# A hybrid decoder block on one core: another division of the first loads and of the memory's scaling, the last left half in two pieces, and another written order

## The chip, the cores and the metric

The kernel runs on one core of a Trainium2 chip. The time is device time in microseconds, the median of several executions; the profile is one further execution, recorded by the hardware profiler.

A core has five engines with a queue each. PE multiplies matrices and writes into PSUM banks. DVE (VectorE) and ACT (ScalarE) work on the elements, POOL (GpSimd) does little of that here, and SP only issues DMAs. POOL and ACT can issue DMAs too, and all of these transfers run on the same 16 DMA engines. Each engine works through its queue in the order in which the program was written, and waits at an instruction until what it reads is there.

## The reference

One layer on 512 tokens of width 1024, all in float32. Three branches read one projection of the normalised input; their gated sum goes through an output projection, then a feed-forward part with a short convolution, then a last norm.

```python
h = rmsnorm(x, norm_mix_g);  proj = h @ w_in            # 1024 x 9216
y_a = (gb * causal_conv3(gc * v)) @ w_a_out             # short gated convolution
u   = causal_conv31(u * sigmoid(ug)) + conv_b_bias      # convolution module
y_b = silu(layernorm(u)) @ w_b_out
k, vm = split(rmsnorm(mem, norm_mem_g) @ w_kv)          # 256 memory rows, 4 heads
y_c = attention(q, k, vm) @ w_att_out
x = x + (sum of sigmoid(gate_i) * y_i) @ w_o
h = rmsnorm(x, norm_ffn_g)
gt, up = split(causal_conv3(h @ w_up))                  # 1024 x 5632
x = x + (silu(gt) * up) @ w_down                        # 2816 x 1024
out = rmsnorm(x, norm_final_g)
```

## The kernel before, in words

**Precision.** A float32 operand is split into a high and a low part that PE takes at its full rate, and each product is three matmuls: high by high, high by low, low by high (`product`, L634 to L636, and `multiply`, L866). A weight therefore passes through four steps before PE can use it: the load, by SP's queue (L713) or by POOL's, which can also add to what is there (L808); the high part on ACT (`whi`, L683); the low part on DVE (`wlo`, L687); the matmuls. There are four buffers for split weights, so the high part of a unit waits until PE is through with the unit four places before it.

**Blocks.** The large projections are cut into "quads", four output blocks that are computed by seven products of sums of blocks in place of eight products. A unit, written (q, f) with f from 1 to 7, is 24 matmuls of 128 by 256. The seven units of a quad share three PSUM banks, and what lies in them is read in seven steps, r1 to r7, by ACT (L893 to L916) and DVE (`add`, L900, and `minus`, L640). Some units add onto a bank that an earlier read has to have seen: unit 6 waits for r1, unit 7 for r6, unit 4 for r7, unit 3 for r5. The usual order of units has another quad's unit between such a pair.

**Stages on PE, in order.** Eleven matmuls of no use to the result that keep PE running while the first loads come (L2105); keys and values of the memory (L1146 and on); the quads of the input projection with the attention between them; the merge of the branches; the output projection (`wo`), the transposes of the normalised rows (`tr`, L1993); eleven quads of the up projection, (up, 0) to (up, 10); the down projection; the end. In the up stage, each pair of quads gives columns of gate (gt) and value (uu). DVE and ACT apply the three taps of the convolution to them (L1654, L1660: into gtc and upc), ACT applies the silu to gtc (L2090), DVE multiplies (z, L2073), and z is split into zh and zl (L2274) for the down projection.

**What sets the order.** The program is a list of jobs (class `Jobs`), each with an engine, a cost, the jobs that it comes after and the buffers that it takes. PE's jobs have a fixed order, that of the list `seq`, in which the table `MOVES` puts single units elsewhere. For all other engines a list scheduler picks the next job by the time at which it could start and then by its due time, which is counted back from PE's order. Two tables shift this per kind of job: `LATER` adds to a due time, `AHEAD` says how long before its due time a job may start at all. `FRESH` names units whose first matmuls write their bank in another pattern. The scheduler's times only set the order; on the chip, semaphores hold each engine.

**The start.** SP loads the memory (two halves, mem), then the keys' first weights (L1081), the values' (L1081) and the next ones. ACT loads its function table (L627), issues the load of 16 columns of norm weights (pk, L628), copies the averaging matrix (mean_w, L629) and scales the four chunks of the first memory half by their norm weights (mg, L954). PE multiplies unsplit float32 there (`keys_product`, L1146), each half of it from two of the chunks.

**The end.** The last of four token blocks is added up in two halves (L2429), squared and summed (L2432), its root taken on ACT (L2453) and inverted on DVE (L2501). Then DVE scales its left 512 columns (L2463) and SP stores them, while ACT scales the right ones (L2459) and stores them on its own queue (L2468).

Of the kernel before, what the change touches and what calls it, by code (L numbers as in the profile page):

```python
# [8 lines left out]
F32 = mybir.dt.float32  # L9
F32R = mybir.dt.float32r  # L10
AF = mybir.ActivationFunctionType
# [3 lines left out]
P = 128  # L15
# [62 lines left out]
    "ACT c3": -190.4, "ACT cf": 13.1, "ACT csq": 651, "ACT exp": -246.7, "ACT fh h b00": -1,  # L78
# [4 lines left out]
    "ACT mg0": 6, "ACT mgh a": 11.9, "ACT mgh b": -6, "ACT mgh c": -22.7, "ACT mgh d": -539,  # L83
    "ACT mgh e": -123, "ACT mgh g": 4, "ACT mh": 472, "ACT mu high": 22, "ACT oh": -68.6,
    "ACT pth": -80, "ACT qh": -60.7, "ACT r1 bb": 75, "ACT r1 cv": 61.8, "ACT r1 gate": 335.4,
# [5 lines left out]
    "ACT sc": -95, "ACT sg": -4.8, "ACT sigmoid": 49, "ACT silu": 91, "ACT sq": -65, "ACT sr": -14,  # L91
    "ACT st": -0.2, "ACT swish": -944, "ACT tap 0": 323, "ACT tap 1": 95, "ACT tap 2": 5,
# [8 lines left out]
    "ACT xg": 33.2, "ACT xroot": -347, "ACT xsquare": 120, "ACT zh a": -186, "ACT zh b": -50,  # L101
    "ACT zh c": -3.4, "ACT zh e": -11, "ACT zh f": -93, "ACT zh g": -0.8, "DVE CV": 16.7,
    "DVE c3": -233, "DVE centre": 100, "DVE cf": 121.1, "DVE csum": -12, "DVE ends": -93.7,
# [6 lines left out]
    "DVE lns": -4.6, "DVE low": -427, "DVE m scale": -18, "DVE mfold": 2, "DVE mfold2": 277,  # L110
    "DVE mgl a": -2.1, "DVE mgl b": -5, "DVE mgl c": -11, "DVE mgl d": 400.7, "DVE mgl g": -334.1,
    "DVE ml": 82, "DVE ms c": -232, "DVE ms e": -2.2, "DVE ms f": 266, "DVE msum": -7,
    "DVE mu fold": -70, "DVE mu low": -150, "DVE mu sum": -187, "DVE ol": 10.7, "DVE pn": -22.2,
# [7 lines left out]
    "DVE sum": 167.8, "DVE tap 0": 898, "DVE tap 1": 336, "DVE tap 2": 0.8, "DVE tap 3": 567,  # L121
    "DVE top": -3576.1, "DVE tot1": 143.2, "DVE tot2": -268.9, "DVE v scale": 78.8,
    "DVE var fold": 114, "DVE var sum": 8, "DVE vl": -9.8, "DVE weigh": -226, "DVE wl K 0": 89.1,
# [8 lines left out]
    "DVE xn": 12.6, "DVE xnorm": -40, "DVE xsum": 40.6, "DVE y t4": -169, "DVE y t5": -5,  # L132
# [9 lines left out]
    "POOL wadd x": -1269, "POOL wadd y": 4, "POOL wl merge 0": 3.3, "POOL wl merge 2": -163.8,  # L142
# [372 lines left out]
def hybrid_block_kernel(  # L515
# [429 lines left out]
    for g in range(2):  # L945
# [1639 lines left out]
```

## Time and profile before

| | before |
| --- | --- |
| median of 3 runs | 918.65 us (918.6 to 918.81) |
| the profiled execution | 918.8 us, of which the span of the trace is 917.0 |
| PE | 908.5 us busy, 99% of the span, 6789 matmuls |
| DVE | 848.7 us, 93% |
| ACT | 684.6 us, 75% |
| POOL | 137.1 us, 15% |
| moved by DMA | 196.91 MB, 215 GB/s |
| granted TensorE clock | 0.999 |

PE is the engine that is nearly always busy, and DVE is next. A row of the timeline gives the start, the duration, the engine, the line and the tiles, and in brackets how long the engine stood idle before it and for what. A row of the waits gives who waited for whom: the sum in us, how often, the longest. A row of the DMA view ends with the size of one transfer and the time from its issue to its landing.

### The profile page before, as it was taken

To read this page: it belongs to the slowest core of one execution; us is meant where nothing else is said; L and a number is where in the kernel's file an instruction comes from. 1 tells how busy PE (TensorE), PEld (TensorE's weight loads), DVE (VectorE), ACT (ScalarE), POOL (GpSimd) and SP (SyncE) were. 2 spreads that over 40 slices of the span, in tenths; PEclk is the share of its full clock that TensorE was granted. 3 is DMA by queue.
4 is the path that set the end of the run, shared out by engine and by line. 5 is a ranking of instruction groups with operands and counts; after the bars stand their busy time and mean duration, and the time that the engine had idled before them with its cause. 6 is when DMAs were issued, how large, how long until landed. Compare 5 with 4: busy or idle time off the path is not lost.

```text
span 917.0 us, 17020 instructions
## 1 busy us (share of the span) xinstructions
PE 908.5 (99%) x6789; PEld 858.7 (94%) x6789; DVE 848.7 (93%) x965; ACT 684.6 (75%) x940; POOL 137.1 (15%) x164
## 2 busy tenths in 40 slices
PE   9999999999999999999999999999999999999997
PEld 8999999999989999999899997899999999988886
DVE  6996999999999999999898989898979899999977
ACT  7777978889988876879748874767757676765566
POOL 0021111101011121110111211121211111002210
PEclk9999999999999999999999999999999999999999
DMA  9999778746769799786958999999999687779962
GB/s 367 371 293 196 153 177 201 157 117 150 212 144 274 167 197 239 151 185 176 227 126 242 204 260 322 260 219 293 276 259 215 143 194 161 191 258 316 270 136 93
DMA packets 55377, 196.91 MB, mean 215 GB/s; under 512 B 6273, under 2 KB 6401, under 8 KB 55297
## 3 DMA queue, kind: packets, MB, share of 16 engines
q0 software_dynamic: 22608, 81.54, 49.4%
q1 hardware_dynamic: 32400, 114.02, 34.3%
q8 instruction: 53, 0.87, 0.4%
q10 hardware_dynamic: 288, 0.27, 0.1%
q14 instruction: 28, 0.22, 0.1%
HBM read 191.60 MB, written 4.19 MB: 214 GB/s over the span
## 4 chain that ended last, share of the span: by engine, by line
PE 99%; DVE 1%; issue 0%; ACT 0%; DVEq 0%
PE bank L866 65%; PE bank L634 7%; PE bank L636 7%; PE bank L635 7%; PE bank L1705 3%; PE bank L1706 3%; PE bank L1704 3%; PE bank L1157 2%; PE bank L1938 1%; PE bank L2105 1%; PE bank L1146 0%; PE bank L1400 0%; PE bank L1993 0%; PE ss L1021 0%; DVE z L2073 0%
## 5 line engine op out<-in xcount | busy, mean ns | idle before, releaser
L683 ACT CAST whi<-wf 128x1024 fp32r<-128x1024 f32 (+1 forms) x197 | 205.2, 1044 | 96.4 <-PE bank L866 48.7
L687 DVE TENSOR_TENSOR wlo<-wf,whi 128x1024 fp32r<-128x1024 f32 (+1 forms) x191 | 230.0, 1213 | 12.3 <-ACT whi L683 12.0
L1472 ACT ACTIVATE tp<-u,pk 128x511 f32<-128x511 f32 (+22 forms) x184 | 119.0, 705 | 6.9 <-DVE acc L1479 5.8
L1479 DVE TENSOR_TENSOR acc<-acc,tp 128x1022 f32<-128x1022 f32 (+22 forms) x92 | 109.4, 1191 | 8.4 <-ACT tp L1472 6.8
L808 POOL DMA_DIRECT2D wf<-in_w_in x43 | 39.4, 938 | 217.0 <-DVE wlo L687 187.2
L866 PE MATMUL bank<-ft4h,whi 128*128 128x256 f32 x248 | 68.6, 277 | 0.9 <-DVE uu L640 0.9
L866 PE MATMUL bank<-fb10h,whi 128*128 128x256 f32 x248 | 68.7, 277 | 0.0
L866 PE MATMUL bank<-fb00h,whi 128*128 128x256 f32 x248 | 68.7, 277 | 0.0
L866 PE MATMUL bank<-ft7h,whi 128*128 128x256 f32 x248 | 68.7, 277 | 0.0
L866 PE MATMUL bank<-ft5l,whi 128*128 128x256 f32 x248 | 68.7, 277 | 0.0
L866 PE MATMUL bank<-fb11h,whi 128*128 128x256 f32 x248 | 68.7, 277 | 0.0
L866 PE MATMUL bank<-ft6l,whi 128*128 128x256 f32 x248 | 68.6, 277 | 0.0
L866 PE MATMUL bank<-ft6h,whi 128*128 128x256 f32 x248 | 68.6, 277 | 0.0
L866 PE MATMUL bank<-ft6h,wlo 128*128 128x256 f32 x248 | 68.6, 276 | 0.0
L866 PE MATMUL bank<-ft7l,whi 128*128 128x256 f32 x248 | 68.6, 276 | 0.0
L866 PE MATMUL bank<-ft5h,whi 128*128 128x256 f32 x248 | 68.6, 276 | 0.0
L866 PE MATMUL bank<-ft5h,wlo 128*128 128x256 f32 x248 | 68.5, 276 | 0.0
L866 PE MATMUL bank<-ft7h,wlo 128*128 128x256 f32 x248 | 68.5, 276 | 0.0
L866 PE MATMUL bank<-fb10l,whi 128*128 128x256 f32 x248 | 68.5, 276 | 0.0
L866 PE MATMUL bank<-fb10h,wlo 128*128 128x256 f32 x248 | 68.5, 276 | 0.0
L866 PE MATMUL bank<-ft4l,whi 128*128 128x256 f32 x248 | 68.5, 276 | 0.0
L866 PE MATMUL bank<-fb00l,whi 128*128 128x256 f32 x248 | 68.5, 276 | 0.0
(418 smaller groups left out, 3172.1 us busy)
## 6 DMA issues: line engine op xcount, KB each, us to landing
wf<-in_w_in SPq DMA_DIRECT2D x50, 512.0 KB, 5.9
wf<-in_w_in POOLq DMA_DIRECT2D x43, 512.0 KB, 6.6
wf<-in_w_up SPq DMA_DIRECT2D x31, 512.0 KB, 6.9
wf<-in_w_up POOLq DMA_DIRECT2D x30, 512.0 KB, 7.2
wf<-in_w_down SPq DMA_DIRECT2D x15, 512.0 KB, 6.1
wf<-in_w_kv SPq DMA_DIRECT2D x8, 512.0 KB, 8.7
wf<-in_w_v SPq DMA_DIRECT2D x8, 512.0 KB, 8.1
wf<-in_w_att_out SPq DMA_DIRECT2D x8, 512.0 KB, 4.1
```

The costliest lines, as they stand in the source:

```text
L634: nc.tensor.matmul(ps, s_hi, w_hi, start=start, stop=False, skip_group_check=again)
L635: nc.tensor.matmul(ps, s_hi, w_lo, start=False, stop=False, skip_group_check=again)
L636: nc.tensor.matmul(ps, s_lo, w_hi, start=False, stop=stop, skip_group_check=again)
L683: nc.scalar.copy(parts[0], src())
L687: nc.vector.tensor_tensor(lo, src(), hi.bitcast(F32), op=ALU.subtract)
L808: nc.gpsimd.dma_start(out=tiles[key], in_=block(w, col[c], k), accum_op=ALU.add)
L866: nc.tensor.matmul(to, w[:, k, at], col, start=first and n == 0, stop=k == 3 and n == 2, skip_group_check=again,)
L1472: nc.scalar.activation(two(("tp", p, s))[:, j, s:], two(("u", p))[:, j, : SEQ - s], AF.Copy, scale=weight(j),)
L1479: nc.vector.tensor_tensor(a, a, two(("tp", p, s))[:, :, s:], op=ALU.add)
L1704: nc.tensor.matmul(ps, w_hi[:, i, at], hi, start=first, stop=False)
L1705: nc.tensor.matmul(ps, w_hi[:, i, at], lo, start=False, stop=False)
L1706: nc.tensor.matmul(ps, w_lo[:, i, at], hi, start=False, stop=last)
```

## The change

Five things are edited.

1. pk's load goes from ACT's queue to POOL's, where it is the first instruction of the kernel's own; the copy of mean_w goes from ACT to DVE.
2. The first load of the keys' weights goes from SP's queue to ACT's, behind the table load in the order of the program.
3. The four chunks of mg are four jobs in place of two: chunks 0 and 2 on ACT, chunks 1 and 3 on DVE. Each half of the keys' product comes after two of them.
4. The left half of the last token block is scaled and stored in two pieces of 256 columns, both by DVE and SP.
5. The tables `LATER`, `AHEAD`, `MOVES` and `FRESH` hold other entries, so the order of nearly all jobs off PE is another, and on PE the order of some units of the up stage and of three transposes.

```diff
 LATER = {
-    "ACT c3": -190.4, "ACT cf": 13.1, "ACT csq": 651, "ACT exp": -246.7, "ACT fh h b00": -1,
+    "ACT cf": 470, "ACT exp": -1067.2, "ACT fh h b00": -451, "ACT fh h b10": -0.1,
...
 FRESH = {
-    (("glu", 2), 7), (("q", 1), 5), (("bb", 0), 7), (("bb", 1), 1), (("gate", 0, 1), 2),
-    (("up", 2), 1), (("up", 0), 5), (("up", 0), 4), (("up", 1), 4), (("up", 2), 6),
+    (("glu", 2), 7), (("q", 1), 5), (("q", 1), 7), (("bb", 0), 7), (("bb", 1), 1),
+    (("gate", 0, 1), 2), (("mq", 1), 3), (("up", 0), 5), (("up", 0), 4), (("up", 1), 7),
+    (("up", 1), 4), (("up", 2), 6),
 }
 MOVES = [
...
-    ((("up", 1), 7), (("up", 1), 4)),
-    ((("up", 1), 2), (("up", 0), 5)),
-    (("tr", 0), ("tr", 1)),
+    (("tr", 2), ("tr", 3)),
+    (("tr", 0), ("wo", "g", 0, 1)),
...
 AHEAD = {
-    "ACT c3": 80, "ACT exp": 80, "ACT fh h b10": 10, "ACT fh h b11": 5, "ACT fh h t5": 10,
+    "ACT csq": 10, "ACT fh h b10": 5, "ACT fh h t4": 150, "ACT fh h t5": 20, "ACT fh h t6": 20,
...
     ident = const.tile([P, P], F32, tag="ident", name="ident")
+    eps = const.tile([P, 1], F32, tag="eps", name="eps")
+    pk = const.tile([P, N_PACKED], F32, tag="pk", name="pk")
+    nc.gpsimd.dma_start(out=pk[:, :N_GAINS], in_=packed[:, :N_GAINS])
     make_identity(nc, ident)
...
     nc.vector.memset(mean_col, 1.0 / D)
+    nc.vector.tensor_copy(mean_w, mean_col.broadcast_to([P, P]))
     nc.scalar.preload_act_table_set("sqrt_and_others")
-    nc.scalar.dma_start(out=pk[:, :N_GAINS], in_=packed[:, :N_GAINS])
-    nc.scalar.copy(mean_w, mean_col.broadcast_to([P, P]))
...
-            def mem_scaled(e=e):
-                if e == 0:
-                    make(("mg0",))
-                for i in range(2 * e, 2 * e + 2):
-                    nc.scalar.activation(
-                        four(("mg0",))[:, i, :], four(("mem", 0))[:, i, :], AF.Copy,
-                        scale=par("norm_mem_g", i),
-                    )
+            def mem_scaled(i):
+                to, t, scale = four(("mg0",))[:, i, :], four(("mem", 0))[:, i, :], par("norm_mem_g", i)
+                if i % 2:
+                    nc.vector.tensor_scalar(to, t, scale, None, op0=ALU.mult)
+                else:
+                    nc.scalar.activation(to, t, AF.Copy, scale=scale)
...
-        job(("ld0", s), "SP", LOAD, lambda: nc.sync.dma_start(out=tiles[raw], in_=src),
-            [("raw tile", s)], LOAD_LATENCY, use=[raw])
+        job(("ld0", s), "SP", LOAD, lambda: (nc.scalar if s == "K" else nc.sync).dma_start(
+            out=tiles[raw], in_=src), [("raw tile", s)], LOAD_LATENCY, use=[raw])
...
-    def left_scaled(t):
-        x1 = late["x1"][t][0]
+    def left_scaled(t, cols=slice(0, SEQ)):
+        x1 = late["x1"][t][0][:, cols]
         nc.vector.scalar_tensor_tensor(
-            x1, x1, r_fin[t], late["g"][0], op0=ALU.mult, op1=ALU.mult
+            x1, x1, r_fin[t], late["g"][0][:, cols], op0=ALU.mult, op1=ALU.mult
         )
...
+        for e, part in enumerate(ENDS if t == last else (slice(0, SEQ),)):
+            job(("sl", t, e), "DVE", 0.37 if t == last else 0.67,
+                lambda t=t, part=part: left_scaled(t, part), [("rc", t)])
+            job(("st", t, 0, e), "SP", STORE, lambda t=t, part=part: stored(t, 0, nc.sync, part),
+                [("sl", t, e)], LOAD_LATENCY)
```

Three places in the order of the program, each as it stands before and as it stands after. A row is one instruction, or several alike (x2), with its line; a number behind a tile's name only tells buffers apart.

ACT's queue at the program's start, before:

```order
L627 ACT_TABLE_LOAD
L628 DMA pk<-in_packed 128x16
L629 CAST mean_w<-mean_col 128x128
L954 ACTIVATE mg_8_118<-mem_95,pk 128x256 x4
L966 CAST mh_129<-mg_8_118 128x512 x2
```

and now, with the keys' weights in the place of pk and half of the chunks:

```order
L626 ACT_TABLE_LOAD
L1080 DMA wf_96<-in_w_kv 128x1024
L952 ACTIVATE mg_6_112<-mem_95,pk 128x256 x2
L961 CAST mh_123<-mg_6_112 128x512 x2
L1090 CAST whi_141<-wf_97 128x512 x2
```

The other two chunks are now the third work on DVE (L950), ahead of its first subtraction.

DVE's queue in the up stage, around the read r7 of (up, 1) (the row that writes uu from a bank), the taps into gtc and upc, z of the first pair of quads, and the low part of unit (up 2, 6) (the first `wlo` row in this piece), before:

```order
L640 SCALAR_TENSOR_TENSOR uu_7438<-bank_6975,uu_7438 128x2x256
L1660 SCALAR_TENSOR_TENSOR gtc_7408<-gt_7066,pk,gtc_7408 128x510
L1660 SCALAR_TENSOR_TENSOR upc_7369<-uu_7267,pk,upc_7369 128x511
L1660 SCALAR_TENSOR_TENSOR upc_7369<-uu_7267,pk,upc_7369 128x510
L687 TENSOR_TENSOR wlo_7473<-wf_7142,whi_7472 128x1024
L2073 TENSOR_TENSOR z<-upc_7369,gtc_7408 128x2x512
L687 TENSOR_TENSOR wlo_7509<-wf_6856,whi_7508 128x1024
```

and now:

```order
L637 SCALAR_TENSOR_TENSOR uu_7406<-bank_6959,uu_7406 128x2x256
L1659 SCALAR_TENSOR_TENSOR gtc_7408<-gt_7064,pk,gtc_7408 128x511
L1659 SCALAR_TENSOR_TENSOR gtc_7408<-gt_7064,pk,gtc_7408 128x510
L1659 SCALAR_TENSOR_TENSOR gtc_7408<-gt_7064,pk,gtc_7408 128x511
L1659 SCALAR_TENSOR_TENSOR gtc_7408<-gt_7064,pk,gtc_7408 128x510
L1659 SCALAR_TENSOR_TENSOR upc_7367<-uu_7235,pk,upc_7367 128x510
L1659 SCALAR_TENSOR_TENSOR upc_7367<-uu_7235,pk,upc_7367 128x511
L1659 SCALAR_TENSOR_TENSOR upc_7367<-uu_7235,pk,upc_7367 128x510
L2072 TENSOR_TENSOR z<-upc_7367,gtc_7408 128x2x512
L684 TENSOR_TENSOR wlo_7502<-wf_7142,whi_7501 128x1024
```

The read of the bank stands ahead of all four taps into gtc instead of ahead of the last, and z stands ahead of the low part of (up 2, 6) instead of behind it. On PE, unit (up 1, 7), whose result r7 reads, stood directly ahead of (up 1, 4) and now stands one unit earlier, ahead of (up 2, 5). On ACT the silu that z waits for stands ahead of the high part of (up 2, 6), which it followed before.

DVE's queue near the end of the up stage, up to r3 of (up, 10) (the row that writes gt from a bank), before:

```order
L687 TENSOR_TENSOR wlo_9503<-wf_9383,whi_9502 128x1024
L2274 TENSOR_TENSOR zl_9564<-z,zh_9560 128x1024
L2073 TENSOR_TENSOR z<-upc_9379,gtc_9474 128x2x512
L687 TENSOR_TENSOR wlo_9583<-wf_9416,whi_9582 128x1024
L687 TENSOR_TENSOR wlo_9557<-wf_9467,whi_9556 128x1024
L1660 SCALAR_TENSOR_TENSOR upc_9586<-uu_9509,pk,upc_9586 128x511
L687 TENSOR_TENSOR wlo_9617<-wf_9447,whi_9616 128x1024
L900 TENSOR_TENSOR gt_9338<-gt_9338,bank_9207 128x2x256
```

and now:

```order
L684 TENSOR_TENSOR wlo_9503<-wf_9348,whi_9502 128x1024
L637 SCALAR_TENSOR_TENSOR z<-z 128x4x256
L2273 TENSOR_TENSOR zl_9566<-z,zh_9558 128x1024
L637 SCALAR_TENSOR_TENSOR z<-z 128x4x256
L684 TENSOR_TENSOR wlo_9581<-wf_9506,whi_9580 128x1024
L684 TENSOR_TENSOR wlo_9561<-wf_9415,whi_9560 128x1024
L684 TENSOR_TENSOR wlo_9614<-wf_9524,whi_9613 128x1024
L1659 SCALAR_TENSOR_TENSOR upc_9585<-uu_9508,pk,upc_9585 128x511
L897 TENSOR_TENSOR gt_9338<-gt_9338,bank_9207 128x2x256
```

The product z of the chunk before, the third row of the first piece, no longer stands here; it is written earlier in the queue. Two sums of z (L637) stand here that stood earlier.

More of the change, by code (lines that the diff above doesn't have):

```diff
@@ new lines @@
+    "ACT fh y t7": -2.4, "ACT high": -4.2, "ACT kh": 6.5, "ACT m root": -60, "ACT mg0": -13,
+    "ACT mgh a": 624, "ACT mgh b": -3, "ACT mgh c": 139.8, "ACT mgh d": 224.7, "ACT mgh g": 231,
+    "ACT mh": 238, "ACT msq": -372.8, "ACT mu high": 79, "ACT pth": -99.7, "ACT r1 bb": -395.5,
[6 rows of a table added]
+    "ACT sigmoid": -2.6, "ACT silu": -186, "ACT sq": -48, "ACT sr": -39, "ACT st": -158,
+    "ACT swish": -889.5, "ACT tap 0": 10.9, "ACT tap 1": 196.2, "ACT tap 2": -200.5,
[9 rows of a table added]
+    "ACT xg": 33.4, "ACT xroot": -141, "ACT xsq": 3.3, "ACT xsquare": -21, "ACT zh a": -322,
@@ new lines @@
+    "ACT zh b": -124.5, "ACT zh c": 17, "ACT zh d": 156, "ACT zh e": 118.3, "ACT zh g": 15.1,
+    "DVE CV": 8.9, "DVE c3": -2535, "DVE centre": 11.5, "DVE cf": 383, "DVE csum": -3,
[6 rows of a table added]
+    "DVE kt": 361.5, "DVE lns": -3.2, "DVE low": -120, "DVE m scale": 194, "DVE mfold": 187,
+    "DVE mfold2": -359.7, "DVE mgl a": 35, "DVE mgl b": 3.6, "DVE mgl c": -235.7, "DVE mgl d": 26.2,
+    "DVE mgl e": -35.6, "DVE mgl g": -1.4, "DVE ml": 3, "DVE ms c": -181.7, "DVE ms d": -47.9,
+    "DVE ms f": -1138, "DVE msum": 836, "DVE mu fold": -484, "DVE mu low": -59.2, "DVE mu sum": 208,
@@ new lines @@
+    "DVE ol": -602, "DVE pn": -694, "DVE ptl": -2738, "DVE ql": -793, "DVE r2 bb": -27,
[6 rows of a table added]
+    "DVE sum": 661.9, "DVE tap 0": 163, "DVE tap 2": -31.6, "DVE tap 3": 1414.3, "DVE top": -2751.7,
+    "DVE tot1": 118, "DVE tot2": 107, "DVE um": 329.9, "DVE v scale": -8, "DVE var sum": -40,
[8 rows of a table added]
+    "DVE x1 g": -263, "DVE xfold": -58.6, "DVE xn": -10, "DVE xnorm": -138.3, "DVE y t4": 79.5,
[8 rows of a table added]
+    "POOL s7 gate": -102, "POOL s7 glu": -189, "POOL s7 up": -73, "POOL wadd e": -208,
+    "POOL wadd x": -280, "POOL wadd y": 2.8, "POOL wl merge 0": -113, "POOL wl merge 2": 4.1,
[6 rows of a table added]
@@ L173 @@
     ((("up", 5), 7), (("up", 7), 1)),
-    ((("up", 4), 3), (("up", 7), 5)),
-    ((("up", 5), 6), (("up", 6), 1)),
-    ((("up", 4), 4), (("up", 6), 5)),
-    ((("up", 4), 7), (("up", 5), 2)),
-    ((("up", 3), 3), (("up", 4), 7)),
-    ((("up", 4), 6), (("up", 5), 1)),
-    ((("up", 3), 4), (("up", 4), 6)),
-    ((("up", 4), 2), (("up", 3), 4)),
-    ((("up", 3), 7), (("up", 4), 2)),
-    ((("up", 3), 6), (("up", 5), 5)),
-    ((("up", 1), 7), (("up", 1), 4)),
-    ((("up", 1), 2), (("up", 0), 5)),
-    (("tr", 0), ("tr", 1)),
+    ((("up", 5), 6), (("up", 7), 5)),
+    ((("up", 4), 3), (("up", 5), 6)),
+    ((("up", 4), 4), (("up", 4), 3)),
+    ((("up", 5), 2), (("up", 4), 4)),
+    ((("up", 3), 3), (("up", 6), 1)),
+    ((("up", 4), 7), (("up", 6), 5)),
+    ((("up", 3), 4), (("up", 4), 7)),
+    ((("up", 4), 6), (("up", 5), 1)),
+    ((("up", 3), 7), (("up", 4), 6)),
+    ((("up", 3), 6), (("up", 4), 2)),
+    (("tr", 2), ("tr", 3)),
+    (("tr", 0), ("wo", "g", 0, 1)),
     ((("mq", 1), 2), (("mq", 1), 6)),
@@ L990, in hybrid_block_kernel @@
             if g == 0:
-                job(("mg0", e), "ACT", 2 * scaled_act(256), mem_scaled,
-                    [("mg0", 0) if e else ("ldm", 0, 0)],
-                    take=[] if e else [(source, ANY)], use=[("mem", 0)] + ([source] if e else []))
-            ready = ([] if e else [("ldm", 1, 0)]) if g else [("mg0", e)]
+                if e == 0:
+                    job(("mg0 tile", 0), "NONE", 0.0, lambda: make(("mg0",)), [("mem tile", 0)],
+                        take=[(source, ANY)])
+                for i in (2 * e, 2 * e + 1):
+                    job(("mg0", i), "DVE" if i % 2 else "ACT", 0.36 if i % 2 else scaled_act(256),
+                        lambda i=i: mem_scaled(i), [("ldm", 0, 0), ("mg0 tile", 0)],
+                        use=[("mem", 0), source])
+            ready = ([] if e else [("ldm", 1, 0)]) if g else [("mg0", 2 * e), ("mg0", 2 * e + 1)]
             job(("mh", g, e), "ACT", 2 * scaled_act(256) if g else actv(512), mem_high,
@@ L1196, in pe_keys @@
                 pe(K0 if e else ("K0",), 4 * MM_WHOLE / 2,
-                   lambda e=e: keys_product(0, 0, (2 * e, 2 * e + 1)), [("ld0", "K"), ("mg0", e)],
+                   lambda e=e: keys_product(0, 0, (2 * e, 2 * e + 1)), [("ld0", "K"), ("mg0", 2 * e), ("mg0", 2 * e + 1)],
                    take=[] if e else [(bank, "ps")],
@@ L2127, in hybrid_block_kernel @@
         for side in sides
-    } | {("mg0", e) for e in range(2)}
+    } | {("mg0", i) for i in range(4)}
     GLU = [("glu", p) for p in range(4)]
@@ L2459, in right_scaled, with stored @@
         nc.scalar.activation(x1, x1, AF.Copy, scale=r_fin[t])
-    def left_scaled(t):
-        x1 = late["x1"][t][0]
+    def left_scaled(t, cols=slice(0, SEQ)):
+        x1 = late["x1"][t][0][:, cols]
         nc.vector.scalar_tensor_tensor(
-            x1, x1, r_fin[t], late["g"][0], op0=ALU.mult, op1=ALU.mult
+            x1, x1, r_fin[t], late["g"][0][:, cols], op0=ALU.mult, op1=ALU.mult
         )
-    def stored(t, i, queue):
+    def stored(t, i, queue, cols=slice(0, SEQ)):
         queue.dma_start(
-            out=out[t * P : (t + 1) * P, i * 512 : (i + 1) * 512], in_=late["x1"][t][i]
+            out=out[t * P : (t + 1) * P, i * 512 + cols.start : i * 512 + cols.stop],
+            in_=late["x1"][t][i][:, cols],
         )
```

44 lines of the change are left out of this document (12 added, 32 removed), and 161 rows, old and new, of tables (AHEAD, LATER).

## The prediction

> **What bounds the kernel now.** I read the page's totals first, then the windows around the first and the last product, then PE's waits, then the timeline and the landings at the places that the diff touches.
>
> ```profile
> span 917.0 us, 17020 instructions
> ...
> PE 908.5 (99%) x6789; PEld 858.7 (94%) x6789; DVE 848.7 (93%) x965; ACT 684.6 (75%) x940; POOL 137.1 (15%) x164
> ```
>
> ```profile
> core 0: us, PE busy (x) PEld busy (x) DVE busy (x) ACT busy (x) POOL busy (x), PEclk, DMA share, GB/s
> 0.00:5.98 5.98, 5.05 (x22) 4.80 (x23) 0.06 (x1) 2.66 (x5) 0.73 (x7) 1.00 0.65 229
> 5.98:910.70 904.72, 903.47 (x6768) 853.87 (x6767) 847.20 (x960) 680.42 (x932) 136.37 (x157) 1.00 0.85 215
> 910.70:917.00 6.30, 0.00 (x0) 0.00 (x0) 1.41 (x4) 1.52 (x4) 0.00 (x0) 0.82 0.57 218
> ```
>
> ```profile
> PE bank L866 <- DVE uu L640: 0.9, 1, 0.9
> PE bank L636 <- DVE zl L2274: 0.4, 1, 0.4
> ```
>
> PE is busy for 903.47 of the 904.72 us from the first real product to the last, at a granted clock of 1.00. The diff takes no product away, so what it can gain is idle PE: the 1.25 us of that long middle, nearly all of it in the two waits shown, and something of the 5.98 us ahead and the 6.30 us behind. Against that, 904 us of a full engine stand open to new waits, since nearly every other queue is written in a new order. The sum is made on this profiled execution: 918.8 us, its span of 917.0 and 1.8 around it. It stands 0.15 above the median of the runs, 918.65. A difference below 0.2% (1.84 us) is taken as no change.
>
> **The start.** The first half of the keys' product (L1146) reads two scaled chunks of the memory (mg); these need the memory (mem) and the norm weights (pk).
>
> ```profile
> 4.90 1.71 ACT L954 ACTIVATE mg<-mem,pk 128x256 f32<-128x256 f32 x4 [2.57 <-DMA pk<-in_packed]
> ...
> 5.95 3.71 PEld L1146 LDWEIGHTS bank<-mg,wf 128*128 128x128 f32 x16 [0.26 <-ACT mg L954]
> ```
>
> ```profile
> L954 ACT ACTIVATE mg<-mem,pk x4: 492/493/507, 4.9 to 6.1; 128x256 f32<-128x256 f32 x4
> ...
> L983 DVE SCALAR_TENSOR_TENSOR ml<-mem,pk,mh x4: 476/478/481, 12.7 to 16.2; 128x256 fp32r<-128x256 f32 x4
> ```
>
> ```profile
> mem<-in_mem_t SPq DMA_DIRECT2D x1, 512.0 KB, 3.9
> wf<-in_w_kv SPq DMA_DIRECT2D x1, 512.0 KB, 4.7
> pk<-in_packed ACTq DMA_DIRECT2D x1, 8.0 KB, 4.0
> ```
>
> ```profile
> 0.74 0.39 SPq L947 DMA_DIRECT2D mem<-in_mem_t  x1
> 0.77 0.39 ACTq L628 DMA_DIRECT2D pk<-in_packed  x1
> ...
> 1.19 0.42 SPq L1081 DMA_DIRECT2D wf<-in_w_kv  x1
> ```
>
> Issue plus landing (the last column of the DMA rows) gives mem at 4.64, pk at 4.8, the keys' weights (wf) at 5.89. ScalarE then scales four chunks in 1.71 us, each 0.49 long, so one per 0.41: the first pair is done at 4.90 + 0.41 + 0.49 = 5.80, and the product begins at 5.98 (the windows above), 0.18 behind it. With the pair split between ScalarE and DVE (0.48 by L983, the nearest DVE row of this shape; DVE has 0.06 us of work before 5.98) the product begins 0.1 + 0.49 + 0.18 = 0.77 behind the last landing. It can come at most 0.26 sooner, the wait of its weight load. So the start breaks even with everything landed by 5.98 - 0.77 = 5.21, and each later us costs a us.
>
> The keys' load leaves at about 0.77 on ScalarE's queue, beside mem, not at 1.19 behind it; all loads behind it on SP move up by its 0.42. But mem then shares the DMA engines. Now the 8 KB of pk, issued 0.03 behind mem on the other queue, needed 4.0 us to mem's 3.9 for 512 KB: the two went forward together. By that, mem and the weights, 1 MB, both end near 5.89, where the same 1 MB ends now: +0.68. If the slow first microseconds are one queue's latency, two queues fill them, and both are there by 5.2: 0. The Trainium skill, page DMA: Bandwidth & Descriptors, section Queues, rings and completion order, has each DMA engine go round the queues with work packet by packet; by that rule the 5.89 holds, and the sum would be 0.2 above mine.
>
> pk on GpSimd's queue has no row. The nearest are weight loads on that queue, its first one and a later one:
>
> ```profile
> ('glu', 0)_60_362<-in_w_in POOLq DMA_DIRECT2D x1, 512.0 KB, 9.5
> ```
>
> ```profile
> ('glu', 2)_100_590<-in_w_in POOLq DMA_DIRECT2D x1, 512.0 KB, 5.8
> ```
>
> 512 KB take 1.25 us (the weights' 5.89 less mem's 4.64), which 8 KB don't need: 5.8 - 1.25 puts pk at 0.75 + 4.5 = 5.3; the first load's 9.5 puts it at 9.0; the 4.0 of ScalarE's queue at 4.8. I take a last landing of 5.7, inside what mem allows and near the quick row for pk: **+0.5 us**, ends -0.26 and +3.8. The same page of the skill, section Anatomy of one DMA — SWDGE (gpsimd) path, fits 2.0 us plus the bytes at 436 GB/s for such a load; no run here shows one so quick, and by it pk is never last. The copy of mean_w on DVE, the identity behind pk's issue on GpSimd (0.73 us of work there before 5.98) and two chunks fewer on ScalarE cost nothing.
>
> **The up stage.** The larger PE wait:
>
> ```profile
> 629.82 0.28 PE L866 MATMUL bank<-ft5l,whi 128*128 128x256 f32 x1
> ...
> 634.35 0.28 PE L866 MATMUL bank<-ft7h,wlo 128*128 128x256 f32 x1
> 635.49 0.39 PE L866 MATMUL bank<-ft4h,whi 128*128 128x256 f32 x1 [0.86 <-DVE uu L640]
> ```
>
> ```profile
> 629.95 2.36 DVE L687 TENSOR_TENSOR wlo<-wf,whi 128x1024 fp32r<-128x1024 f32 x2
> 632.22 2.19 DVE L1660 SCALAR_TENSOR_TENSOR gtc<-gt,pk,gtc 128x511 f32<-128x511 f32 x3
> 634.74 0.69 DVE L640 SCALAR_TENSOR_TENSOR uu<-bank,uu 128x512 f32<-128x512 f32 x1 [0.33 <-PE bank L866]
> 635.35 0.74 DVE L1660 SCALAR_TENSOR_TENSOR gtc<-gt,pk,gtc 128x510 f32<-128x510 f32 x1
> 636.01 1.53 DVE L1660 SCALAR_TENSOR_TENSOR upc<-uu,pk,upc 128x511 f32<-128x511 f32 x2
> 637.45 1.22 DVE L687 TENSOR_TENSOR wlo<-wf,whi 128x1024 fp32r<-128x1024 f32 x1
> 638.59 1.22 DVE L2073 TENSOR_TENSOR z<-upc,gtc 128x1024 f32<-128x1024 f32 x1
> ```
>
> ```profile
> 636.17 1.28 ACT L2090 ACT_TABLE_LOAD   x1 [0.83 <-DVE gtc L1660]
> 637.46 1.06 ACT L2090 ACTIVATE gtc<-gtc 128x1024 f32<-128x1024 f32 x1
> ```
>
> Products start 0.113 apart here (634.35 less 629.82, over 40), so 635.49 stands 1.03 behind its place at 634.46: unit (up 1, 4) waits until DVE has read the bank of (up 1, 7), computed just ahead. In the new order (up 2, 5), 24 products or 2.72 us, lies between the two, DVE reads that bank ahead of the taps, and the wait is gone: -1.03. What is late next is unit (up 2, 6), 48 products on: it could begin at 634.46 + 5.44 = 639.90, but its weights' low part (wlo) now stands behind z on DVE, and z behind silu on ScalarE. DVE: the bank's read at 632.3, 0.6; four taps of gtc at 0.73 to 635.8; three of upc to 638.0. ScalarE: table and silu 2.35 behind gtc, 638.2 (now 638.5). Then z, 1.14, and wlo, about 1.2: 640.5, 0.6 late. If the weights' high part slips behind the silu, it is ready by 639.2 and decides nothing. Net: **-0.5 us**, ends -1.03 and 0 (0 when the rest of it comes back). At the head of the stage, transposes 0 and 2 and the first units change places; a transpose moved ahead of a product of the output projection covers a wait of 0.1: **-0.1**, ends -0.1 and +0.2.
>
> **The down stage.** The smaller wait:
>
> ```profile
> 813.51 0.68 DVE L900 TENSOR_TENSOR gt<-gt,bank 128x512 f32<-128x512 f32 x1
> ...
> 823.65 1.82 DVE L2274 TENSOR_TENSOR zl<-z,zh 128x768 fp32r<-128x768 f32 x2
> ```
>
> ```profile
> 823.86 0.42 PE L635 MATMUL bank<-wlo,zh 128*128 128x512 f32 x1
> 824.66 0.50 PE L636 MATMUL bank<-whi,zl 128*128 128x512 f32 x1 [0.37 <-DVE zl L2274]
> ```
>
> From the read of the last gate bank (L900) to zl, DVE works through eleven steps without a pause, so zl comes as early as that read starts. The same steps follow it in the new order, but z of the chunk before and the low part ahead of it stand earlier; counted in the durations above, the read starts about 0.5 sooner. PE's products here are twice as wide as those that start 0.113 apart, so 824.66 is 0.80 - 0.23 = 0.57 late: **-0.4**, ends -0.57 and +0.3, the latter if a weight's low part that now stands behind it is the late one.
>
> **The tail.** After the last product nothing overlaps.
>
> ```profile
> 912.23 0.75 DVE L2463 SCALAR_TENSOR_TENSOR x<-x,cols,gfin 128x512 f32<-128x512 f32 x1
> 912.99 0.38 ACTq L2468 DMA_DIRECT2D out<-x  x1
> ```
>
> ```profile
> out<-x ACTq DMA_DIRECT2D x1, 256.0 KB, 2.8
> out<-x SPq DMA_DIRECT2D x1, 256.0 KB, 2.6
> ```
>
> Both last stores leave near 913.0; the later landing is 912.99 + 2.8 = 915.8. In two pieces (0.48 each, as L983) the first store leaves at 912.7, 0.28 sooner, the second at 913.1, 0.13 later. A quarter of the 512 KB (0.31 us) is thus moved out of the common stretch: **-0.3**, ends -0.35 and +0.13.
>
> **The rest of the order.** No products change place elsewhere, but some third of the steps on DVE, ScalarE, SP and GpSimd do. PE idles so little in the middle that there is next to nothing to gain; a step that now comes late costs as the two waits do, 0.4 to 1.0 each. I take one small one, **+0.3**, ends 0 and +2.
>
> Sum: 0.5 - 0.5 - 0.1 - 0.4 - 0.3 + 0.3 = -0.5, so 918.3 for the profiled execution and 918.15, rounded 918.2, for the median.
>
> **The rivals.**
> - Every gain and no cost: -0.26 - 1.03 - 0.1 - 0.57 - 0.35 = -2.3, or 916.3. For it: PE's two waits are what the new order goes round. Against it: a start that needs three loads on three queues by 5.0, and z ahead of wlo.
> - The gains come back: the wait of 1.03 moves to (up 2, 6) whole, the down stage keeps its own. Then 0.5 - 0.1 - 0.3 + 0.3 = +0.4: 919.0.
> - Slower: pk on GpSimd's queue is as late as that queue's first load. PE stands still until 9.0 + 0.77, +3.8 in place of +0.5: 921.5. It makes the kernel slower by over 1.84 from a landing near 8.0 on. For it: the one first load of that queue in the trace. Against it: that load shared DMA engines that were full.
> - New waits in the re-sorted queues, three or more, +2 or more in place of +0.3: 919.9 and up.
>
> **How the numbers follow.** My sum 0.50; every gain 0.13; gains back 0.13; pk late 0.12; new waits 0.12. Of these, faster by over 0.2% (below 916.8) are most of the second and a little of the first, 0.15; slower (above 920.5) most of pk late and half of the new waits, 0.16; the rest, 0.69, is no change. The sum's own range is 917.2 to 919.3. The range for 8 in 10 runs from 916.6, near the full gain, to 920.3, where pk lands near 7.8 or two or three new waits come together.
>
> **What would show it.** Right: the keys' product (L1146 now) starts at 6.2 to 6.8, held by mg; no PE wait of 0.9 near 634, but 0.5 or so within 6 us behind; a PE wait under 0.2 near 823; 6.0 us from the last product to the span's end. Wrong: the product after 7.5 and mg waiting for pk; PE waits over 0.3 at places that had none; or a middle whose idle PE is still 1.2.

## The result and the profile after

The changed kernel takes 920.34 us in the median of 13 runs (918.53 to 922.28); 13 runs of the kernel before, among them the three shown above, have 918.81 (918.37 to 920.74). The ratio is 1.0017 with an interval of 1.0009 to 1.0025: slower by about 1.5 us, where 0.5 us faster was forecast. That is under the 0.2% below which the prediction counts no change, but 920.34 lies 0.04 above its range of 916.6 to 920.3. The 13 runs of the changed kernel fall into groups: two near 918.5, seven from 920.1 to 920.6, four from 921.7 to 922.3.

The profiled execution of the changed kernel took 920.07 us, with a span of 918.3. Its totals:

```profile
span 918.3 us, 17053 instructions
...
PE 908.4 (99%) x6789; PEld 858.1 (93%) x6789; DVE 849.2 (92%) x969; ACT 684.3 (75%) x937; POOL 138.1 (15%) x165
```

All of PE's waits:

```profile
PE bank L1145 <- ACT mg L952: 2.4, 1, 2.4
PE bank L2104 <- DVE mean_col L624: 0.9, 1, 0.9
PE bank L863 <- ACT gt L890: 0.4, 1, 0.4
```

The wait of 0.9 on uu is gone, the one of 0.4 on zl is below the list, and one of 2.4 us has come at the very start. The landings of the first loads (the last column, us from the issue) and their issues show why:

```profile
mem<-in_mem_t SPq DMA_DIRECT2D x1, 512.0 KB, 5.2
wf<-in_w_kv ACTq DMA_DIRECT2D x1, 512.0 KB, 5.4
wf<-in_w_v SPq DMA_DIRECT2D x1, 512.0 KB, 6.3
pk<-in_packed POOLq DMA_DIRECT2D x1, 8.0 KB, 5.6
```

```profile
0.75 0.38 SPq L944 DMA_DIRECT2D mem<-in_mem_t  x1
0.78 0.39 ACTq L1080 DMA_DIRECT2D wf<-in_w_kv  x1
...
1.28 0.70 POOL L612 DMA_DIRECT2D pk<-in_packed  x1 [0.83 <-POOLq L2575]
...
6.86 0.91 ACT L952 ACTIVATE mg<-mem,pk 128x256 f32<-128x256 f32 x2 [4.84 <-DMA pk<-in_packed]
6.86 0.62 DVE L950 TENSOR_SCALAR mg<-mem,pk 128x256 f32<-128x256 f32 x2 [5.73 <-DMA pk<-in_packed]
7.42 2.64 PEld L1145 LDWEIGHTS bank<-mg,wf 128*128 128x128 f32 x7 [2.56 <-ACT mg L952]
7.42 2.93 PE L1145 MATMUL bank<-mg,wf 128*128 128x256 f32 x6 [2.37 <-ACT mg L952]
```

mem is there at 5.95 in place of 4.64, the keys' weights at 6.2 in place of 5.89, and pk, the last, at 6.86. The scaling starts with pk, the product 0.56 behind it at 7.42: 1.44 us later than before.

That is about half of what the start loses. In the last row, six matmuls take 2.93 us (this view ends at 10 us; all sixteen take 5.33). Before, sixteen took 4.08, and the first product of split operands followed at 9.71:

```profile
5.98 4.08 PE L1146 MATMUL bank<-mg,wf 128*128 128x256 f32 x16
...
9.71 0.58 PE L634 MATMUL bank<-whi,mh 128*128 128x512 f32 x1
```

The same split product in the changed kernel:

```profile
12.41 0.58 PE L631 MATMUL bank<-whi,mh 128*128 128x512 f32 x1
```

Two windows of PE in the changed kernel (us, then PE's busy time and matmuls, and near the row's end the granted clock, 0.57 and 0.50):

```profile
7.00:11.00 4.00, 3.58 (x9) 2.92 (x10) 3.16 (x7) 4.00 (x8) 0.00 (x0) 0.57 1.04 425
8.00:10.00 2.00, 2.00 (x6) 1.63 (x5) 1.69 (x3) 2.00 (x5) 0.00 (x0) 0.50 1.02 418
```

PE had idled for 2.4 us, and it then ran at half its clock. The trace's record of the granted clock, which that column sums up, has three entries here: full from 3.90, half from 7.31, full again from 10.72 us, so two stretches of 3.41 us. The split product, the next one behind the slow matmuls, comes 2.70 us later than before, of which 1.44 are the wait and 1.26 the slow matmuls.

The record has no entry ahead of its first full one, and the column counts time without an entry as 1.00. The matmuls themselves show that PE starts at half rate in every profile here: the ones of no use start 0.21 us apart until that first entry and 0.11 apart after it, those of the keys' product 0.43 and then 0.215. PE's first matmul starts at 0.93 in all ten profiles, but the first entry comes at 3.90 in this one, at 6.79 in that of before, in between in seven others, and at 11.74 in the tenth, told below (5 first matmuls). So the twenty-two records of the matmuls of no use (two for each of the eleven) take more or less time from one execution to the next. Before, and then in the changed kernel:

```profile
0.93 5.06 PE L2105 MATMUL bank<-mean_col 128*128 128x128 f32 x22 [0.93 <-DVE mean_col L626]
```

```profile
0.93 4.13 PE L2104 MATMUL bank<-mean_col 128*128 128x128 f32 x22 [0.93 <-DVE mean_col L624]
```

The keys' product of before also ran at half rate up to 6.79, so it took 3.73 us to the split product, where six profiles in which the clock was full by then took 3.34 to 3.37. Against those the half-clock stretch costs the changed kernel about 1.6.

In the up stage the forecast place of the next wait shows it. PE and ACT:

```profile
642.58 0.39 PE L863 MATMUL bank<-ft6h,whi 128*128 128x256 f32 x1 [0.40 <-ACT gt L890]
```

```profile
637.80 1.28 ACT L2089 ACT_TABLE_LOAD   x1 [3.67 <-DVE gtc L1659]
639.10 1.06 ACT L2089 ACTIVATE gtc<-gtc 128x1024 f32<-128x1024 f32 x1
640.07 1.99 ACT L680 CAST whi<-wf 128x1024 fp32r<-128x1024 f32 x2
641.96 0.57 ACT L890 COPY gt<-bank 128x512 f32<-128x512 f32 x1
```

(up 1, 4) no longer waits; (up 2, 6) starts 0.57 us behind its place. The down stage's wait and the two last stores:

```profile
825.62 0.39 PE L632 MATMUL bank<-wlo,zh 128*128 128x512 f32 x1
826.14 0.50 PE L633 MATMUL bank<-whi,zl 128*128 128x512 f32 x1
```

```profile
914.27 0.81 SPq L2467 DMA_DIRECT2D out<-x  x2
914.51 0.35 ACTq L2467 DMA_DIRECT2D out<-x  x1
```

The gap there is 0.52 - 0.23 = 0.29 in place of 0.57. The last matmul started at 910.40, 6.64 us ahead of the span's end at 917.04; now it starts at 911.92, 6.38 ahead of 918.30.

### The profile page after: what moved, and what is told of

It is laid out like the page before. It is cut to its first block, busy times and chain, and to the rows that moved or that the text cites. A ratio compares the mean times of both kernels' runs of the same rounds, so it can differ in the third digit from the quotient of the medians.

```text
span 918.3 us, 17053 instructions
## 1 busy us (share of the span) xinstructions
PE 908.4 (99%) x6789; PEld 858.1 (93%) x6789; DVE 849.2 (92%) x969; ACT 684.3 (75%) x937; POOL 138.1 (15%) x165
## 4 chain that ended last, share of the span: by engine, by line
PE 95%; DVE 2%; issue 1%; ACT 1%; DMA 1%; DVEq 0%; ACTq 0%; POOLq 0%
PE bank L863 62%; PE bank L633 6%; PE bank L631 6%; PE bank L632 6%; PE bank L1703 3%; PE bank L1704 3%; PE bank L1705 3%; PE bank L1156 2%; DVE wlo L684 1%; PE bank L1937 1%; DVE gtc L1659 1%; DMA pk<-in_packed 1%; PE bank L1145 1%; ACT whi L680 0%; PE bank L1992 0%
## 5 line engine op out<-in xcount | busy, mean ns | idle before, releaser
L1478 DVE TENSOR_TENSOR acc<-acc,tp 128x1018 f32<-128x1018 f32 (+22 forms) x92 | 109.1, 1188 | 6.6 <-ACT tp L1471 4.7
L863 PE MATMUL bank<-fb11l,whi 128*128 128x256 f32 x248 | 68.5, 276 | 0.0
L863 PE MATMUL bank<-ft4h,wlo 128*128 128x256 f32 x248 | 68.5, 276 | 0.0
```

Of the source, the lines that this page charges most:

```text
L863: nc.tensor.matmul(to, w[:, k, at], col, start=first and n == 0, stop=k == 3 and n == 2, skip_group_check=again,)
L1478: nc.vector.tensor_tensor(a, a, two(("tp", p, s))[:, :, s:], op=ALU.add)
```

## Experiments

Each is told with its edit, its expectation as written ahead of the run, and what came. Medians and ratios are against runs of the kernel before on the same chip in the same call: 918.28 us for the first four, 918.41 for the last four.

**Only pk moved.** The kernel before, pk's load on GpSimd's queue:

```diff
+    nc.gpsimd.dma_start(out=pk[:, :N_GAINS], in_=packed[:, :N_GAINS])
     make_identity(nc, ident)
...
-    nc.scalar.dma_start(out=pk[:, :N_GAINS], in_=packed[:, :N_GAINS])
```

> The kernel before with one edit: pk's first load on GpSimd's queue, ahead of the identity. Theory (the late pk and the slow clock behind PE's idle time make the whole loss): pk lands near 6.8, ScalarE scales from there, the keys' product starts near 7.7 in place of 5.98, PE is idle about 2 us and the granted clock falls to 0.5 for some us behind it, so the kernel is 1.7 to 4.0 us slower than before: about 921 to 922. Rival (the memory, slowed by the keys' weights on a second queue, is what is late): mem still lands at 4.6 here, and the start loses less than 1 us.

919.16 us, ratio 1.0008 (0.9999 to 1.0017): less than expected. Its first loads and PE's wait:

```profile
mem<-in_mem_t SPq DMA_DIRECT2D x1, 512.0 KB, 3.7
wf<-in_w_kv SPq DMA_DIRECT2D x1, 512.0 KB, 4.5
pk<-in_packed POOLq DMA_DIRECT2D x1, 8.0 KB, 4.7
```

```profile
PE bank L1146 <- ACT mg L954: 0.6, 1, 0.6
```

With one queue beside it, pk takes 4.7 us in place of the 5.6 beside two, and is there at 1.27 + 4.7 = 6.0. The product starts at 6.59, 0.61 later than before. PE idles for only 0.6 us, and the product runs at full rate. The split product is 0.25 later than before, and by 50 us PE stands 0.80 behind; what lies between was not followed up. So pk alone is late, but this expectation's price was too high: the other part of pk's lateness comes with the keys' load on a second queue.

**Only the keys' load left on a second queue.** The changed kernel with pk at the head of SP's queue:

```diff
-    nc.gpsimd.dma_start(out=pk[:, :N_GAINS], in_=packed[:, :N_GAINS])
...
     nc.scalar.preload_act_table_set("sqrt_and_others")
+    nc.sync.dma_start(out=pk[:, :N_GAINS], in_=packed[:, :N_GAINS])
```

> The changed kernel with pk's first load on SP's queue, first of all and ahead of mem; the keys' weights stay on ScalarE's queue beside mem. It tells the two causes of the late start apart. If sharing costs by itself: pk lands below 5, mem near 6 to 6.4, the product starts near 6.9 and the kernel is 0.5 to 1.0 slower than with both loads back. If only pk was late: mem lands by 5, and the start is 6.0 or earlier.

917.64 us, ratio 0.9993 (0.9984 to 1.0002), 0.4 above the kernel with both loads back below, compared through the kernel before of each call 0.3.

```profile
wf<-in_w_kv ACTq DMA_DIRECT2D x1, 512.0 KB, 3.9
mem<-in_mem_t SPq DMA_DIRECT2D x1, 512.0 KB, 4.8
pk<-in_packed SPq DMA_DIRECT2D x1, 8.0 KB, 2.9
```

```profile
6.61 3.72 PE L1145 MATMUL bank<-mg,wf 128*128 128x256 f32 x16 [1.37 <-ACT mg L952]
```

mem, now issued behind pk, lands at about 6.0, the keys' weights at 4.7: of the two loads on two queues one comes as early as mem came before and the other as late as the second one did. Here that is the wrong one of them, since the scaling stands between mem and the product: +0.63 at the product. But mem also leaves 0.43 later here, at 1.18, so this run doesn't separate sharing cleanly. The changed kernel does for mem: it leaves at 0.75 as before and lands 1.31 later beside the keys' load. In the time, the 0.3 is not clear of noise, since the intervals of the two kernels overlap.

**pk back on ScalarE's queue, the keys' weights behind it there.**

```diff
-    nc.gpsimd.dma_start(out=pk[:, :N_GAINS], in_=packed[:, :N_GAINS])
...
     nc.scalar.preload_act_table_set("sqrt_and_others")
+    nc.scalar.dma_start(out=pk[:, :N_GAINS], in_=packed[:, :N_GAINS])
```

> The changed kernel with pk back on ScalarE's queue alone, ahead of the keys' weights there; these still go beside mem on a second queue. Theory: mem and the weights land near 6.0 to 6.2, pk no later, the product starts near 6.8 with PE idle 1 us or less, and the kernel stands 0.5 to 1.0 above the one with both loads back, 917.9 to 918.4; the granted clock stays at 1.00. Rival (two queues fill the start): the product starts by 6.0 and this is as fast as with both loads back. Rival (mem on shared engines is the whole loss): as slow as the changed kernel.

918.7 us, ratio 1.0006 (0.9997 to 1.0015), slower than expected.

```profile
mem<-in_mem_t SPq DMA_DIRECT2D x1, 512.0 KB, 3.7
wf<-in_w_v SPq DMA_DIRECT2D x1, 512.0 KB, 5.5
wf<-in_w_kv ACTq DMA_DIRECT2D x1, 512.0 KB, 6.3
pk<-in_packed ACTq DMA_DIRECT2D x1, 8.0 KB, 3.9
```

```profile
7.58 3.69 PE L1145 MATMUL bank<-mg,wf 128*128 128x256 f32 x16 [1.66 <-DMA wf<-in_w_kv]
```

Now mem and pk are as early as before, and the keys' weights come at about 7.5, behind pk on their own queue and beside the values' weights on SP's. The product starts at 7.58, later than in the changed kernel. But the kernel is about 1 us faster than that one in the median (ratios 1.0006 and 1.0017, whose intervals overlap a little). In the profiled execution PE, idle for 1.7 us, keeps its clock: sixteen matmuls in 3.69 us. Not every execution does: the four longest of the eleven, 920.0 to 920.9, have a mean granted clock of 0.996 or 0.997, the other seven, 918.4 to 918.8, one of 0.998 or 0.999.

**Both loads back.** pk as in the last diff, and:

```diff
-        job(("ld0", s), "SP", LOAD, lambda: (nc.scalar if s == "K" else nc.sync).dma_start(
+        job(("ld0", s), "SP", LOAD, lambda: nc.sync.dma_start(
```

> The changed kernel with both first loads put back (pk on ScalarE's queue, the keys' weights on SP's behind mem); chunks on two engines, tail in two pieces and the new order stay. Theory: the start is that of before or up to 0.26 earlier, the clock stays at 1.00, and what is left are the gains of the order and the tail: 0.5 near 634, 0.3 near 823, 0.3 in the tail, so 1.0 to 1.5 us faster than before, about 917.4. Rival (the new order itself loses): 918.6 or more.

917.24 us, ratio 0.9989 (0.9980 to 0.9997): faster than before by 1.0 us, as expected. Beside the wait of 0.9 ahead of the first matmuls, PE's waits are

```profile
PE bank L1145 <- DMA wf<-in_w_kv: 0.9, 1, 0.9
PE bank L863 <- ACT gt L890: 0.4, 1, 0.4
```

The product starts at 5.98 as before. With the chunks on two engines it no longer waits for them but for the weights, which land at 5.89; so their division alone moves nothing. Chunks, order and tail as a whole gain; the two loads are what made the change a loss (0.9989 against 1.0017). The profiled execution, 918.69, is one of the longer ones of its eleven; the last section shows why.

**The order alone.** The kernel before with the four tables of the changed one (`LATER`, `AHEAD`, `MOVES`, `FRESH`) in the place of its own.

> The kernel before with the four tables of the changed one and nothing else: the order alone. Theory: PE waits 0.57 near 640 and 0.3 near 823 in place of 1.02 and 0.57, the start and the tail are those of before, so 0.7 us faster than before. Rival (the new order has small stalls that eat its gain): within 0.2 us of before, with idle PE of over 1.2 us in the middle.

917.54 us, ratio 0.9989 (0.9980 to 0.9998): 0.9 us faster than before, with 0.7 expected. The two waits have the predicted sizes, 0.57 and 0.33 by the starts of PE's products. The profile of this kernel has one more, a wait of 1.2 us of an up unit with f = 4 for its weights' high part, at 624.1, which neither the changed kernel nor the one with both loads back shows. That execution took 918.88, the second longest of its eleven. Whether others have the wait is not shown, and what brought it on stays open.

**More matmuls ahead of the product.** The changed kernel, loads and order as they are:

```diff
-        for i in range(11):
+        for i in range(17):
             nc.tensor.matmul(ps[:, :P], some, some, start=True, stop=True)
```

> The changed kernel with 17 in place of 11 of the first matmuls that keep PE running (their results are not used), order and loads unchanged. Theory (a part of the loss is the half clock behind PE's idle time): the product still starts near 7.4, but the idle time ahead of it falls from 2.4 us to about 1, the granted clock stays at 1.00 from 7 to 11 us, and the kernel is about 1.2 us faster than the changed one, 919.0. Rival (the wait alone is the loss, the clock costs nothing): the same time as the changed kernel.

918.65 us, ratio to before 1.0004 (0.9996 to 1.0013), against the changed kernel's 1.0017 (1.0009 to 1.0025): 1.2 us faster, as expected. The intervals just touch, but nine of its eleven runs lie at 918.4 to 918.8, and only two of the changed kernel's thirteen. PE's wait for mg and the window of 8 to 10 us:

```profile
PE bank L1145 <- ACT mg L952: 0.8, 1, 0.8
```

```profile
8.00:10.00 2.00, 2.00 (x11) 1.76 (x10) 1.57 (x3) 2.00 (x5) 0.00 (x0) 1.00 1.02 418
```

The product starts at 7.54, even later than in the changed kernel, and eleven matmuls run in the 2 us in which six ran there. PE's idle time ahead of them is another, 0.8 in place of 2.4 us, and the clock, full from 4.73 here, is not halved again.

**Fewer matmuls ahead of the product.** The kernel before with the suspected cost alone:

```diff
-        for i in range(11):
+        for i in range(5):
             nc.tensor.matmul(ps[:, :P], some, some, start=True, stop=True)
```

> The kernel before with 5 in place of 11 of the first matmuls whose results are not used; loads and order unchanged. The suspected cost alone: the product's inputs come at the same time, but PE idles about 2.5 us ahead of 5.98. Theory (idle time of that length brings the half clock): the product still starts near 5.98, the granted clock falls to about 0.5 for 3 to 4 us, and the kernel is 1 to 2 us slower. Rival (the clock has nothing to do with it): the same time as before.

921.26 us in the median of 6 runs, ratio 1.0028 (1.0017 to 1.0040): 2.9 us slower, more than expected, though the product starts at 6.05, 0.07 later than before. In the second row, 15 of the sixteen matmuls are counted, since the view ends at 12 us.

```profile
0.93 2.50 PE L2105 MATMUL bank<-mean_col 128*128 128x128 f32 x10 [0.93 <-DVE mean_col L626]
6.05 6.28 PE L1146 MATMUL bank<-mg,wf 128*128 128x256 f32 x15 [2.62 <-DMA wf<-in_w_kv]
```

```profile
8.00:10.00 2.00, 2.00 (x6) 1.57 (x5) 1.99 (x4) 2.00 (x4) 0.00 (x0) 1.00 1.01 416
```

Six matmuls in 2 us is half rate again. The column of the granted clock says 1.00 here only because the record has no entry yet: its first, full, comes at 11.74. So the theory named the wrong step. The clock did not fall behind the idle time; it had not yet risen, as the five matmuls of no use ended at about 3.4 us and ran at half rate to the last, and the product stayed at half rate until 11.74. The cost is of the same kind as in the changed kernel, a product at half clock, with no load changed; but what this run shows is what too few matmuls ahead cost, and not what an idle time does to a clock that is already full.

**A version that beats both.** Both loads back, and the keys' first weights loaded in two halves, so that each half of the product waits only for its own:

```diff
+        def first_load():
+            for at in ENDS_K if s == "K" else (slice(0, 1024),):
+                nc.sync.dma_start(out=tiles[raw][:, at], in_=src[:, at])
+
-        job(("ld0", s), "SP", LOAD, lambda: nc.sync.dma_start(
-            out=tiles[raw], in_=src), [("raw tile", s)], LOAD_LATENCY, use=[raw])
+        job(("ld0", s), "SP", LOAD, first_load, [("raw tile", s)], LOAD_LATENCY, use=[raw])
```

Here `ENDS_K` is the two halves of the 1024 columns.

> The kernel with both first loads put back, and the keys' first weights loaded in two halves of 256 KB, each half of the product waiting only for its own. Theory: the product waits for the weights there (5.89) and not for the chunks (5.4), so the first half lands near 5.3 and the product starts near 5.6, 0.3 to 0.4 earlier, where the first matmuls are through by then; 916.9. Rival (the matmuls at half rate ahead of it end only at 5.98): no change.

916.76 us, ratio 0.9984 (0.9975 to 0.9993): the lowest median of all, 1.6 us below before. Against the kernel with both loads back (0.9989) the gain is not clear of noise.

```profile
5.78 3.85 PE L1149 MATMUL bank<-mg,wf 128*128 128x256 f32 x16
```

The product starts with no wait right where the first matmuls end, 0.20 earlier. That is less than the 0.3 to 0.4 hoped for; in this execution, whose clock is full only from 6.25, those matmuls are what bounds it.

## Why the prediction was wrong

**The start**, forecast at +0.5 us, came at +2.70, and it alone turned the sign. Two steps of it failed.

The first is the last landing, a size. The working had it at 5.7, "inside what mem allows and near the quick row for pk"; it was pk at 6.86. Two pieces of this were mis-sized. pk left GpSimd at 1.28, not at 0.75, after 0.83 us in which that engine waited for its own queue, which no row of the profile before shows for a load so early. And it took 5.6 us, not 4.5: 4.7 with only SP's queue loaded beside it, 5.6 with SP's and ScalarE's. I had put the two edits side by side as if the later of them alone counted; but the keys' load on a second queue made pk later too. The sentence on mem held: both loads end near where the same 1 MB ended before, 5.95 and 6.2 against the 5.89 of the working, of which the 5.7 stayed short. Of the 3.8 us that the rival "pk late" asked for, 1.44 came. The way from the landing to the product was read too long, which hid a part of this: 0.56 in the changed kernel, not 0.77. The working took the 0.18 between the first two chunks and the product of before as part of that way; but there the weights landed (5.89) and the matmuls of no use ended (5.98) at nearly the same time, and with both loads back and the chunks earlier the product still starts at 5.98.

The rule of the Trainium skill, page DMA: Bandwidth & Descriptors, section Queues, rings and completion order, that was set beside this (each DMA engine goes round the queues packet by packet) agrees with the changed kernel, where both loads of 512 KB took 5.2 and 5.4 us. With pk ahead on SP the two didn't end together: 4.7 and 6.0, where the keys' load had left 0.40 earlier. The section Anatomy of one DMA — SWDGE (gpsimd) path of the same page of the Trainium skill, with its 2.0 us and little more for pk, is not what the runs show: 4.7 and 5.6.

The second is the step "each later us costs a us". It leaves out the clock. PE that idles for 0.6 (pk alone) or 1.4 us (pk on SP) loses no more than that at the product; in the changed kernel PE idles for 2.4 us, and its next matmuls run at half rate, 1.26 us more. With 17 matmuls of no use the product starts no earlier, but PE idles for 0.8 us, the half rate is gone, and the kernel is 1.2 us faster. The run with 5 of them shows the same price from the other side: PE is not yet at full rate when the product starts, and 2.9 us are lost with the product 0.07 later. The prediction read the eleven matmuls of no use as cover that was given, and never asked what becomes of the clock when their cover ends 2 us too soon.

The mean granted clock, on record for nearly every run, bears this out beyond the profiled ones (it leaves out the time ahead of the first entry). It is 0.996 or 0.997 in nine of the changed kernel's thirteen runs, all of 920 us or more, and in the four longest with pk back on ScalarE's queue, where PE idled for 1.7 us in the profiled run; in all other runs that have it, it is 0.998 or more. The changed kernel's two shortest runs, near 918.5, have 0.998. Two of its longer runs have 0.999, and what made these long is not shown.

On its page TensorE: Matmul & The Clock Gate, section Part 1: The HAM clock gate, the Trainium skill says that TensorE runs at half clock until it has been busy for a window of about 3.4 us, and goes back after an idle one, and that these windows run on regardless of the kernel. The half rate and the length agree: the changed kernel's record changes at 3.90, 7.31 and 10.72 us, 3.41 apart. But its clock fell after a stretch in which PE had still been busy for 1.15 us, so the window need not be idle as a whole. That the windows run on regardless of the kernel fits the first full entries, from 3.90 to 6.79 us in nine profiles whose PE starts alike. It would also say why the same kernel pays in one run and not in another; with one profile of the changed kernel, that last step is argued, not shown.

**The up stage**, forecast at -0.5: right in size and place. The wait of 1.03 went and 0.57 came back six microseconds on, at the unit named. But by the profile what came last there was not the step named, so the close agreement (0.57 and 0.6) is in part luck: it was the read r1 of (up, 2), the copy at 641.96 (L890), behind silu and two high parts on ScalarE; the low part on DVE, which the working named, is done at about the same time, since the two steps of DVE behind z run from 641.34 for 2.36 us and the first of them is the one needed. r1 could not have gone ahead of z: in the program's list it comes after it. The -0.1 at the stage's head came: between 585 and 607 us, PE's matmuls gain about 0.15 on those of before.

**The down stage**, forecast at -0.4: 0.57 became 0.29, so -0.3, most of it given away 22 us earlier, where the first products of the down stage start late and PE falls behind by 0.24. Net it is about -0.1.

**The tail**, forecast at -0.3: -0.26 in the changed kernel, and -0.27 to -0.39 in the other five profiles with two pieces (6.25 to 6.37 in place of 6.64): right.

**The rest of the order**, forecast at +0.3: beside what is named, PE shows no gap over 0.15 us in the changed kernel that it didn't show before. The order alone gained 0.9 us in the median, so the 0.3 charged for new waits was not needed.

Put together by the starts of PE's matmuls: +2.70 at the start, about -0.6 for the order from there to the end, -0.26 in the tail, and -0.6 that are no gain of the change. These come from a stretch in the profile of before, told in the last section. The sum is +1.3, which is the difference of the spans, 918.3 - 917.0.

The rival "pk late" had the right load and the right direction, without the clock, and was given 0.12. Its price was worked out from the first load of 512 KB and was too high, and its point of decision (a landing near 8.0) was too late, since the clock was left out.

## What to carry to other kernels

Price an idle PE at the start by what follows it as well. In this kernel 0.6 to 1.4 us of it cost only themselves; with 1.7 us the clock on record is lower in four of eleven runs, with 2.4 us in nine of thirteen, and there the wait was paid nearly twice. A few more matmuls of no use bought the second half back. Two loads that are both needed first gained nothing from two queues here, where the DMA engines are full from about 3 us on (a share of 0.93 to 1.09 in each microsecond from 3 to 7 in the changed kernel). Order them by what stands behind each, and try splitting the one that the first product waits for. A small load on GpSimd's queue is not small in time: 4.7 to 5.7 us for 8 KB at the program's start, issued half a microsecond late, against 3.9 to 4.3 on ScalarE's queue.

## What had not been expected of the hardware

PE has stretches in which it runs some 4% slower while the granted clock reads 1.00 and DVE keeps its pace (0.88 us a step in both rows below). The same products of the up stage, in the same window, in the kernel with both loads back and in the one with 17 first matmuls:

```profile
642.00:685.00 43.00, 43.00 (x367) 42.94 (x366) 36.83 (x42) 27.28 (x34) 9.65 (x11) 1.00 1.03 259
```

```profile
642.00:685.00 43.00, 43.00 (x382) 43.00 (x381) 37.70 (x43) 28.27 (x36) 10.06 (x12) 1.00 1.05 266
```

15 matmuls of 0.113 us are missing in the first, 1.7 us. The profile of before has such a stretch from 608 to 624, with 138 matmuls where the same kernel with pk moved has 144; this is the -0.6 of the sum above. The run with 5 first matmuls has one there too (137), so three of the ten profiles show it. The programs don't differ there in PE's work, so one profile can hold a microsecond that belongs to the execution and not to the kernel. What brings these stretches on stays open.
